# Column sums of all eight squares on TensorE, a re-ordered prologue, and work issued behind named instructions, in a four-layer backbone

## The chip, the cores and the metric

The kernel runs on one core of one Trainium2 chip. The metric is the device time of one execution in microseconds (us). The engines are named as in the profile: PE (TensorE, matrix products; PEld is its weight load), DVE (VectorE), ACT (ScalarE), POOL (GpSimd) and SP (SyncE, which issues most of the DMA transfers).

## What is computed

512 tokens, 256 of context (`ctx`) and 256 latent (`x`), of 1024 channels pass through four layers. Each layer has a token mixer (layer 0 latent attention, layer 1 a Conformer convolution, layer 2 a Hyena long convolution, layer 3 latent attention again) and a gated feed-forward network (FFN) with a convolution over three neighbours. Ahead of each mixer and each FFN the tokens are normed and modulated:

```python
def rmsnorm(x, g):
    y = xf * lax.rsqrt(jnp.mean(xf * xf, axis=-1, keepdims=True) + EPS)
    return (y * g.astype(F32)).astype(x.dtype)
def modulate(x, g, shift, scale):
    return rmsnorm(x, g) * (1 + scale) + shift
...
    sh1, sc1, g1, sh2, sc2, g2 = jnp.split(s_lat @ ada_w[i] + ada_b[i], 6, axis=-1)
    csh1, csc1, cg1, csh2, csc2, cg2 = jnp.split(s_ctx @ ada_w[i] + ada_b[i], 6, axis=-1)
    hl = modulate(x, norm_mix[i], sh1, sc1)
    ...
    x = x + g1 * yl
    x = x + g2 * conv_ffn(modulate(x, norm_ffn[i], sh2, sc2), *ffn)
def conv_ffn(h, w_up, w_dw, b_dw, w_down):
    g = dwconv(a[..., :D_FF], w_dw, b_dw)          # a = h @ w_up
    return (jax.nn.silu(g) * a[..., D_FF:]) @ w_down
```

The shifts and scales are products of the conditioning vectors with `ada_w` (1024 x 6144 for each layer). The Hyena filter (two sine layers, a decay, the discrete Fourier transform of the filter, and the sum of its absolute values by which it is divided) depends on weights alone, so it can be computed at any time before layer 2.

## The kernel before, in words

The tokens are kept transposed, `x[128, KT=8, 512]`: 8 tiles of 128 channels by 512 tokens, the context in columns 0 to 255 (`s=0`), the latent tokens behind (`s=1`). Every float32 operand of a product is split into a high part (ACT copies it rounded, L144, L169, L385) and a low part (DVE subtracts, L147, L170, L166 for `hl`); a product is three matmuls, hi by hi, lo by hi, hi by lo (`mm3`, L158 to L160). Weights come as 1 MB tiles `raw` through SP's queue and are split into `whi` and `wlo`.

The order on PE is written by hand (`tc.manual_schedule`). The order on DVE, ACT, POOL and SP is made by a scheduler from the program's order, priorities, and the buffers that are free when it plans: 35 buffers for tiles `g` and `e`, 4 for `raw`, 11 for `w`, 7 PSUM banks for `mm`. An engine carries its instructions out strictly in that order.

**The prologue** is the time until layer 0's attention begins. It holds: the modulation of layer 0 (`ada_group(0, 0)`, eight slices k of 1 MB of `ada_w`, four products each, L243; k=2 to 4 in two tiles `aw`; one step for each `fill()`); its eviction (ACT L248), four transposes and the bias (`settle()`, L260, L262); the sine layers (`spectra`: products L1144 and L1157, sines L1100 to L1107) with four column products L1151 for the Conformer filter, whose results `ka` go to DRAM (`spill`); the first half of the Hyena filter (`spectra_half(0, ...)`: for two halves t of the filter taps L1171 to L1185, then spectra columns `fcol`, six products each, L1195); the sums of squares of the tokens. `piece()` takes the next step of the last two, and `warm_up(n)` issues n idle products (L221).

For the norm, ACT squares the eight tiles of x (L335), DVE adds the first seven (L337, six adds), and `Norm.sums(s)` multiplies the accumulated tile and the eighth with a column of ones (L357; 128 tokens become one column, four products for each s). ACT adds eps (`tv`, L360), POOL takes the power -1/2 (`rsy`, L195), ACT lays it on a diagonal (L364), PE spreads it over the partitions (L368, `spread`). `Norm.apply(s)` scales x (DVE L166, `e<-x,moda,mm`), adds the shift (ACT L385, `hh`) and takes the low part (`hl`).

**Layer 0's head** (`mla`): four weight tiles `w_c` (two halves of two, `whi`, `wlo`), products of `hh` of the context with them for k = 0 to 7 (L636), `nm.sums(1)` between k=3 and k=4, products of `hl` (L642), the latent tokens' `spread` behind the first eight of these, then the latent tokens' products.

**Each FFN** has 22 units j: six pairs of weight tiles' products (L158 to L160) into two banks, then `post(j)`: a scaled eviction (ACT L528), two taps (DVE L166 `e<-mm,par,e`), silu (L533), the product (DVE L534) and a split (L169, L170). After some units `down(gi)` multiplies back and adds to x (DVE L166 `x<-mm,mod,x`). Beside it `ada_side` computes the next layer's modulation on DVE and ACT: eight products L284 and eight accumulations L285 for each tile. In layer 1's FFN, which is called the second FFN here, the second half of the Hyena filter is computed as well: `spectra_half(1, ...)`, one step every second unit.

Of the kernel before, what the change touches and what calls it, by code (L numbers as in the profile page):

```python
# [16 lines left out]
ALU = mybir.AluOpType  # L17
# [5 lines left out]
T = 512  # L23
# [60 lines left out]
def kernel(ctx: ExitStack, tc: tile.TileContext, xT, cT, cB, ada0, ada2, adaT1, adaT2, adaT3, prm, mlp, w_c, w_ug, w_o,  # L84
# [80 lines left out]
    def stt(o, a, s, b, op0, op1, **kw):  # L165
        nc.vector.scalar_tensor_tensor(out=o, in0=a, scalar=s, in1=b, op0=op0, op1=op1, **kw)  # L166

    def split(hi, lo, src):
        nc.scalar.activation(out=r(hi), in_=src, func=AF.Copy)  # L169
        nc.vector.tensor_tensor(out=r(lo), in0=src, in1=hi, op=ALU.subtract)  # L170

# [58 lines left out]
    def ada_group(li, g, early=False):  # L230
        mod_tile(li)
        ps = pa.tile([P, T], F32, tag="ada", name="ada")
        for k in range(KT):
            if early and k in (2, 3, 4):
                raws = [wp.tile([P, 1024], F32, tag="w", name="aw", bufs=WB) for _ in range(2)]
            else:
                raws = [wp.tile([P, 2048], F32, tag="raw", name="raw", bufs=RAW)]
            n = 4 // len(raws)
            for i, raw in enumerate(raws):
                at = (4 * g + n * i) * T  # L240
                nc.sync.dma_start(out=raw, in_=(ada0, None, ada2)[li][k * P:(k + 1) * P, at:at + n * T])
            for c in range(4):
                nc.tensor.matmul(out=ps[32 * c:32 * c + 32, :], lhsT=spad[:, k, :], rhs=raws[c // n][:, c % n * T:(c % n + 1) * T],  # L243
                                 start=(k == 0), stop=(k == KT - 1))
            if k < KT - 1:
                yield
        sb = e_tile()
        nc.scalar.activation(out=sb, in_=ps, func=AF.Copy)  # L248
        late.append((li, g, sb))
        yield  # L250

    late = []

# [64 lines left out]
    def need(n):  # L318
        while units[0] < n:
            was = units[0]  # L320
            fill()
            if units[0] == was:
                break

    class Sq:
        def __init__(self, c0, eng=nc.gpsimd):
            self.c0, self.acc, self.n, self.parts, self.eng = c0, None, [0, 0], {}, eng

        def add(self, k, a, b):
# [16 lines left out]
    class Norm:  # L346
# [6 lines left out]
        def sums(self, s):  # L353
            ps = ps_tr()
            for t in range(2):
                for i, q in enumerate(self.sq.parts[s]):
                    nc.tensor.matmul(out=ps[:, t:t + 1], lhsT=q[:, s * L + t * P:s * L + (t + 1) * P], rhs=ones[:, 0:1],  # L357
                                     start=i == 0, stop=i == 1)
            v = sp.tile([P, 2], F32, tag="tv", name="tv")
# [10 lines left out]
        def apply(self, s):  # L370
# [5 lines left out]
            if self.a is None:  # L376
                self.a = sp.tile([P, KT, 2], F32, tag="moda", name="moda")
                stt(self.a, self.m[:, self.c + 8:self.c + 16, :], 1.0, self.g.unsqueeze(2).to_broadcast([P, KT, 2]),
                    ALU.add, ALU.mult)
            hs = []  # L380
            shift = lambda k: self.m[:, self.c + k, s:s + 1]
            for k in range(KT):
                hs.append(e_tile()[:, v])
                stt(hs[k], x[:, k, v], self.a[:, k, s:s + 1], R[:, v], ALU.mult, ALU.mult)
                nc.scalar.activation(out=r(HH[:, k, v]), in_=hs[k], func=AF.Identity, bias=shift(k))  # L385
            with tc.high_priority(offset=-18 if s == 0 else 0):
# [194 lines left out]
    def mla(li, nm):  # L581
# [6 lines left out]
        for u in range(2):  # L588
            w += [both(t, lambda a: a.rearrange("p (k c) -> p k c", k=2)) for t in load_w(w_c[j, u], 2 * CW, 2 * CW)]
        if li == layers[0]:  # L590
# [570 lines left out]
    def spectra_half(hc, loaded):  # L1161
# [4 lines left out]
        fwd = lambda t, a, b: (fh[t][:, a:b], fl[t][:, a:b])  # L1166
        ab, asum = [], []
        for t in range(2):
# [11 lines left out]
            split(hl4[0], hl4[1], s)  # L1180
            split(hl4[2], hl4[3], d)
            ab.append(((hl4[0], hl4[1]), (hl4[2], hl4[3])))
            stt(f, f, -1.0, f, ALU.mult, ALU.max)
            stt(b, b, -1.0, b, ALU.mult, ALU.max)
            nc.vector.tensor_tensor(out=f, in0=f, in1=b, op=ALU.add)  # L1185
            asum.append(f)
            yield
        kf = [[e_tile(), e_tile()] for _ in range(2)]
        for fcol, w in ((0, 0), (1, 0), (2, 1), (3, 1)):
# [4 lines left out]
            for j in range(2):  # L1194
                nc.scalar.activation(out=kf[j][f2][:, im * L:(im + 1) * L], in_=ps[:, j * L:(j + 1) * L], func=AF.Copy)  # L1195
            if fcol % 2:
                yield
# [164 lines left out]
    with tc.manual_schedule(engines={mybir.EngineType.PE}):  # L1362
        filler[0] = chain(ada_group(0, 0, True), ada_group(0, 1), ada_group(0, 2), ada_group(2, 0))
        la, lb = spectra_load()
        pieces = chain(spectra(la), spectra_half(0, lb))
        sq = Sq(0, nc.vector)
        nm = Norm(layers[0], 0, sq)
        def piece():
            kas.extend(next(pieces) or ())
# [3 lines left out]
        for k in (0, 4):  # L1373
            nc.sync.dma_start(out=x[:, k:k + 4, :], in_=xT[:, k:k + 4, :])
        for k in range(KT):
            sq.add(k, 0, T)
        for i in range(3):
            piece()
        warm_up(12)
        fill()  # L1380
        for i in range(2):
            piece()
            warm_up(6)
            fill()
        nm.sums(0)
        fill(3)
        piece()
        settle()
        piece()
        nm.apply(0)  # L1390
        spare[0] = pieces
# [168 lines left out]
```

## Time and profile before

| | us |
|---|---|
| median of 3 runs (lowest, highest) | 2145.23 (2144.37, 2145.5) |
| the profiled execution | 2145.16 |
| its span in the profile | 2143.3 |
| PE busy, share of the span | 2096.1, 98% |
| DVE busy, share | 1557.3, 73% |
| ACT busy, share | 1287.5, 60% |
| mean granted clock of PE | 0.994 |

The span is what the rows below divide; 1.86 us of the profiled execution lie outside it. A row of a timeline gives start, duration, engine, line, operation, tiles (output <- inputs) and count, and in brackets how long the engine had stood idle and whose end released it.

### The profile page before, as it was taken

To read this page: it belongs to the slowest core of one execution; us is meant where nothing else is said; L and a number is where in the kernel's file an instruction comes from. 1 tells how busy PE (TensorE), PEld (TensorE's weight loads), DVE (VectorE), ACT (ScalarE), POOL (GpSimd) and SP (SyncE) were. 2 spreads that over 40 slices of the span, in tenths; PEclk is the share of its full clock that TensorE was granted. 3 is DMA by queue.
4 is the path that set the end of the run, shared out by engine and by line. 5 is a ranking of instruction groups with operands and counts; after the bars stand their busy time and mean duration, and the time that the engine had idled before them with its cause. 6 is when DMAs were issued, how large, how long until landed. Compare 5 with 4: busy or idle time off the path is not lost.

```text
span 2143.3 us, 32063 instructions
## 1 busy us (share of the span) xinstructions
PE 2096.1 (98%) x12108; PEld 1801.3 (84%) x12108; DVE 1557.3 (73%) x2780; ACT 1287.5 (60%) x2774; POOL 236.2 (11%) x403
## 2 busy tenths in 40 slices
PE   7999999999999999999999999999999998899999
PEld 5767898888899979888888988898888888669999
DVE  5878368889756665768775689757979856976665
ACT  3788457778644465547654544456868745875453
POOL 0375200000020012000000200020000002621000
PEclk8999999999999999999999999999999999999999
DMA  8533135545432152444542322224545531114552
GB/s 316 211 131 139 60 118 179 214 177 200 173 128 84 59 205 81 155 150 163 196 171 85 114 85 93 99 79 158 210 182 196 197 113 50 58 46 171 180 189 85
DMA packets 48699, 305.39 MB, mean 142 GB/s; under 512 B 5536, under 2 KB 6688, under 8 KB 16160
## 3 DMA queue, kind: packets, MB, share of 16 engines
q1 hardware_dynamic: 47824, 300.91, 39.8%
q8 instruction: 95, 1.56, 0.3%
q10 hardware_dynamic: 720, 2.44, 0.3%
q14 instruction: 60, 0.49, 0.1%
HBM read 299.13 MB, written 4.19 MB: 142 GB/s over the span
## 4 chain that ended last, share of the span: by engine, by line
PE 89%; DVE 4%; ACT 3%; POOL 2%; DMA 1%; issue 1%; SPq 0%; POOLq 0%; ACTq 0%; DVEq 0%
PE mm L158 26%; PE mm L159 25%; PE mm L160 25%; PE mm L463 4%; PE mm L469 2%; PE mm L850 1%; PE ada L243 1%; PE tr L829 1%; PE mm L636 1%; ACT g L761 1%; DMA x<-in_xT_dram 1%; PE tr L357 1%; PE idle L221 1%; POOL e L337 1%; PE mm L642 0%
## 5 line engine op out<-in xcount | busy, mean ns | idle before, releaser
L158 PE MATMUL mm<-hh,whi 128*128 128x512 f32 (+1 forms) x1856 | 657.2, 354 | 0.0
L159 PE MATMUL mm<-hl,whi 128*128 128x512 f32 (+1 forms) x1856 | 654.5, 353 | 0.0
L160 PE MATMUL mm<-hh,wlo 128*128 128x512 f32 (+1 forms) x1856 | 654.2, 352 | 0.0
L147 DVE TENSOR_TENSOR wlo<-raw,whi 128x1024 fp32r<-128x1024 f32 (+2 forms) x361 | 430.0, 1193 | 290.4 <-PE mm L159 179.2
L144 ACT ACTIVATE whi<-raw 128x1024 fp32r<-128x1024 f32 (+3 forms) x370 | 374.6, 1017 | 293.9 <-PE mm L160 160.7
L158 PEld LDWEIGHTS mm<-hh,whi 128*128 128x128 f32 x1856 | 351.1, 189 | 51.7 <-issue 3.1
L160 PEld LDWEIGHTS mm<-hh,wlo 128*128 128x128 f32 x1856 | 351.0, 189 | 47.7
L159 PEld LDWEIGHTS mm<-hl,whi 128*128 128x128 f32 x1856 | 351.2, 189 | 46.3
L285 ACT ACTIVATE e<-e 128x512 f32<-128x512 f32 x512 | 315.9, 619 | 80.8 <-DVE e L284 80.5
L284 DVE TENSOR_TENSOR e<-raw,e 128x512 f32<-128x512 f32 x512 | 315.3, 684 | 0.0
L158 PE MATMUL mm<-g,whi 128*128 128x512 f32 (+1 forms) x904 | 309.1, 342 | 0.0
L159 PE MATMUL mm<-g,whi 128*128 128x512 f32 (+1 forms) x904 | 307.5, 340 | 0.0
L160 PE MATMUL mm<-g,wlo 128*128 128x512 f32 (+1 forms) x872 | 298.5, 342 | 0.0
L337 POOL TENSOR_TENSOR e<-e 128x256 f32<-128x256 f32 (+1 forms) x63 | 70.2, 1114 | 1209.7 <-ACT e L335 1176.6
L158 PEld LDWEIGHTS mm<-g,whi 128*128 128x128 f32 x904 | 171.3, 189 | 19.7
L159 PEld LDWEIGHTS mm<-g,whi 128*128 128x128 f32 x904 | 171.3, 190 | 19.6
L160 PEld LDWEIGHTS mm<-g,wlo 128*128 128x128 f32 x872 | 165.3, 190 | 19.0
L169 ACT ACTIVATE g<-e 128x512 fp32r<-128x512 f32 (+1 forms) x137 | 76.3, 558 | 106.4 <-DVE e L534 45.3
L166 DVE SCALAR_TENSOR_TENSOR e<-mm,par,e 128x510 f32<-128x510 f32 (+3 forms) x186 | 126.2, 678 | 15.6 <-ACT e L528 11.6
L166 DVE SCALAR_TENSOR_TENSOR x<-mm,mod,x 128x256 f32<-128x256 f32 x192 | 85.3, 477 | 52.0 <-PE mm L160 51.8
L170 DVE TENSOR_TENSOR g<-e,g 128x512 fp32r<-128x512 f32 (+1 forms) x137 | 81.9, 598 | 41.8 <-ACT g L169 41.4
L528 ACT ACTIVATE e<-mm,par 128x512 f32<-128x512 f32 (+1 forms) x88 | 63.0, 716 | 63.7 <-PE mm L160 59.2
(264 smaller groups left out, 2856.1 us busy)
## 6 DMA issues: line engine op xcount, KB each, us to landing
raw<-in_w_fup_dram SPq DMA_DIRECT2D x88, 1024.0 KB, 4.9
raw<-in_adaT_dram SPq DMA_DIRECT2D x64, 1024.0 KB, 4.8
raw<-in_w_fd_dram SPq DMA_DIRECT2D x32, 1024.0 KB, 4.9
raw<-in_ada_dram SPq DMA_DIRECT2D x29, 1024.0 KB, 5.2
raw<-in_w_fd_dram SPq DMA_DIRECT2D x16, 768.0 KB, 4.2
raw<-in_w_p_dram SPq DMA_DIRECT2D x12, 1024.0 KB, 4.9
raw<-in_w_hi_dram SPq DMA_DIRECT2D x12, 1024.0 KB, 5.0
raw<-in_w_o_dram SPq DMA_DIRECT2D x8, 1024.0 KB, 4.9
```

The source lines that it names most:

```text
L144: nc.scalar.activation(out=r(hi[:, 0:n]), in_=part, func=AF.Copy)
L147: nc.vector.tensor_tensor(out=r(lo[:, 0:n]), in0=part, in1=hi[:, 0:n], op=ALU.subtract)
L158: nc.tensor.matmul(out=ps, lhsT=r(ah), rhs=r(bh), start=start, stop=False)
L159: nc.tensor.matmul(out=ps, lhsT=r(ah), rhs=r(bl), start=False, stop=False)
L160: nc.tensor.matmul(out=ps, lhsT=r(al), rhs=r(bh), start=False, stop=stop)
L166: nc.vector.scalar_tensor_tensor(out=o, in0=a, scalar=s, in1=b, op0=op0, op1=op1, **kw)
L169: nc.scalar.activation(out=r(hi), in_=src, func=AF.Copy)
L170: nc.vector.tensor_tensor(out=r(lo), in0=src, in1=hi, op=ALU.subtract)
L284: nc.vector.tensor_tensor(out=t, in0=raw[:, q * D + (i % 2) * T:q * D + (i % 2 + 1) * T], in1=sb[i], op=ALU.mult)
L285: nc.scalar.activation(out=t, in_=t, func=AF.Copy, accum_out=asum[:, 2 * u + q, i // 2, i % 2:i % 2 + 1])
L337: self.eng.tensor_tensor(out=self.acc[:, a:b], in0=self.acc[:, a:b], in1=t[:, a:b], op=ALU.add)
L463: nc.tensor.matmul(out=banks[i][q][:, v], lhsT=r(wq[:, k, :]), rhs=r(HH[:, k, v]), start=k == 0 and wq is w[i][q][0], stop=False)
```

## The change

`Sq.all` squares the eight tiles on ACT and hands all eight to `Norm.sums`; the six adds on DVE are gone, and `sums` has 16 products instead of 4 for each s. In the prologue, PE's order is written anew. The splits of the four `w_c` tiles may be issued only behind marked instructions (`tc.issue_after`: the eviction of the modulation and the second scaled tile for the first pair, the last `hh` of the context for the second). In `spectra_half`, for both halves of the filter, the absolute values are issued only behind the last split of t=1 (mark "parts"). In the first half, each spectra column is a step of its own.

```diff
+        def all(self):
+            tiles = []
+            for k in range(KT):
+                tiles.append(e_tile())
+                nc.scalar.activation(out=tiles[k], in_=x[:, k, :], func=AF.Square)
+            self.parts = {0: tiles, 1: tiles}
...
-                for i, q in enumerate(self.sq.parts[s]):
+                qs = self.sq.parts[s]
+                for i, q in enumerate(qs):
                     nc.tensor.matmul(out=ps[:, t:t + 1], lhsT=q[:, s * L + t * P:s * L + (t + 1) * P], rhs=ones[:, 0:1],
-                                     start=i == 0, stop=i == 1)
+                                     start=i == 0, stop=i == len(qs) - 1)
...
-            w += [both(t, lambda a: a.rearrange("p (k c) -> p k c", k=2)) for t in load_w(w_c[j, u], 2 * CW, 2 * CW)]
+            with queued(*((("evict", "scaled"), ("apply",))[u] if li == layers[0] else ())):
+                w += [both(t, lambda a: a.rearrange("p (k c) -> p k c", k=2)) for t in load_w(w_c[j, u], 2 * CW, 2 * CW)]
...
-            split(hl4[2], hl4[3], d)
+            marks["parts"] = split(hl4[2], hl4[3], d).ins
             ab.append(((hl4[0], hl4[1]), (hl4[2], hl4[3])))
-            stt(f, f, -1.0, f, ALU.mult, ALU.max)
-            stt(b, b, -1.0, b, ALU.mult, ALU.max)
-            nc.vector.tensor_tensor(out=f, in0=f, in1=b, op=ALU.add)
-            asum.append(f)
+            fb.append((f, b))
             yield
+        with queued("parts"):
+            for f, b in fb:
+                stt(f, f, -1.0, f, ALU.mult, ALU.max)
+                stt(b, b, -1.0, b, ALU.mult, ALU.max)
+                nc.vector.tensor_tensor(out=f, in0=f, in1=b, op=ALU.add)
+                asum.append(f)
...
-            if fcol % 2:
+            if fcol % 2 or hc == 0:
                 yield
...
-        for k in range(KT):
-            sq.add(k, 0, T)
         for i in range(3):
             piece()
-        warm_up(12)
+        warm_up(10)
+        piece()
+        sq.all()
         fill()
-        for i in range(2):
-            piece()
-            warm_up(6)
-            fill()
+        piece()
+        warm_up(4)
+        fill(2)
         nm.sums(0)
-        fill(3)
         piece()
+        fill()
+        piece()
+        fill(2)
+        warm_up(4)
         settle()
+        nm.spread(0)
+        nm.apply(0)
         piece()
-        nm.apply(0)
+        piece()
         spare[0] = pieces
```

The order on PE around the sums of the context (names: `ada` is the modulation, `aw` and `raw` its slices, `idle` the warm-up, `g` the filter's split parts). Before:

```order
L221 MATMUL idle<-ones,ident 128x128 x6
L243 MATMUL ada<-aw,spad 32x512 x4
L357 MATMUL tr<-ones,e 128x1 x4
L243 MATMUL ada<-raw,spad 32x512 x12
L158 MATMUL mm<-g 128x512
L159 MATMUL mm<-g 128x512
L160 MATMUL mm<-g 128x512
```

Of the change (its L373 is L357 of before):

```order
L243 MATMUL ada<-aw,spad 32x512 x8
L373 MATMUL tr<-ones,e 128x1 x16
L158 MATMUL mm<-g 128x512
L159 MATMUL mm<-g 128x512
L160 MATMUL mm<-g 128x512
L158 MATMUL mm<-g 128x512
L159 MATMUL mm<-g 128x512
L160 MATMUL mm<-g 128x512
L243 MATMUL ada<-raw,spad 32x512 x4
```

The products with ones have grown from 4 to 16 and stand ahead of the last three slices of the modulation; two spectra columns stand among these slices.

The two last spectra columns now stand behind the spread (L384, before L368):

```order
L243 MATMUL ada<-raw,spad 32x512 x8
L221 MATMUL idle<-ones,ident 128x128 x4
L262 MATMUL tr<-ident,e 128x128 x4
L384 MATMUL mm<-e,ones 128x256
L158 MATMUL mm<-g 128x512
```

In before all spectra columns stood ahead of the spread.

The order on ACT up to the context's `hh` (L385). Before:

```order
L144 ACTIVATE whi<-raw 128x832
L364 ACTIVATE e<-ident,rsy 128x128 x2
L248 ACTIVATE e<-ada 128x512
L1195 ACTIVATE e<-mm 128x256 x4
L144 ACTIVATE whi<-raw 128x832 x2
L1195 ACTIVATE e<-mm 128x256 x2
L144 ACTIVATE whi<-raw 128x832
L1195 ACTIVATE e<-mm 128x256 x2
L385 ACTIVATE hh<-e,mod 128x256 x7
```

Of the change (L404 is L385 of before, L1219 is L1195):

```order
L248 ACTIVATE e<-ada 128x512
L144 ACTIVATE whi<-raw 128x832
L404 ACTIVATE hh<-e,mod 128x256 x2
L1219 ACTIVATE e<-mm 128x256
L404 ACTIVATE hh<-e,mod 128x256 x5
L1219 ACTIVATE e<-mm 128x256
L404 ACTIVATE hh<-e,mod 128x256
L1219 ACTIVATE e<-mm 128x256 x2
L144 ACTIVATE whi<-raw 128x832 x3
```

Three of the four splits of `w_c` (`whi`) now stand behind the last of the eight `hh`, and the spectra's copies stand among the `hh`.

The order on DVE in the second FFN, around the last updates of x of its first `down` (`x<-mm`); the last row is the first low part for unit j=10. Before:

```order
L166 SCALAR_TENSOR_TENSOR x<-mm,mod,x 128x256 x6
L170 TENSOR_TENSOR g<-e,g 128x512
L284 TENSOR_TENSOR e<-raw,e 128x512 x15
L166 SCALAR_TENSOR_TENSOR x<-mm,mod,x 128x256
L284 TENSOR_TENSOR e<-raw,e 128x512
L166 SCALAR_TENSOR_TENSOR x<-mm,mod,x 128x256
L284 TENSOR_TENSOR e<-raw,e 128x512 x8
L147 TENSOR_TENSOR wlo<-raw,whi 128x1024
```

Of the change (L554 is L534 of before, L286 is L284, L1210 is L1185):

```order
L554 TENSOR_TENSOR e<-e,mm 128x512
L166 SCALAR_TENSOR_TENSOR x<-mm,mod,x 128x256 x2
L170 TENSOR_TENSOR g<-e,g 128x512
L286 TENSOR_TENSOR e<-raw,e 128x512 x24
L166 SCALAR_TENSOR_TENSOR e<-e 128x512
L166 SCALAR_TENSOR_TENSOR e<-mm,par,e 128x2x255
L1210 TENSOR_TENSOR e<-e 128x512
L166 SCALAR_TENSOR_TENSOR e<-mm,par,e 128x2x255
L147 TENSOR_TENSOR wlo<-raw,whi 128x1024
```

The x updates stand ahead of all 24 products of `ada_side`, and between these and `wlo` there are now an absolute value and a sum (`e<-e`, L1210) and the taps of unit j=9.

## Rows read from the trace of the kernel before

**Rows 1.** the page's first part: busy us, share of the span, instructions:

```profile
PE 2096.1 (98%) x12108; PEld 1801.3 (84%) x12108; DVE 1557.3 (73%) x2780; ACT 1287.5 (60%) x2774; POOL 236.2 (11%) x403
```

**Rows 2.** the middle: length, PE, PEld, DVE, ACT, POOL busy, clock, DMA share, GB/s:

```profile
950.00:1000.00 50.00, 50.00 (x222) 41.42 (x221) 35.07 (x54) 27.65 (x69) 0.00 (x0) 1.00 0.41 139
```

**Rows 3.** chain that ended last: start us, us, what:

```profile
5.30 13.95 DMA x<-in_xT_dram
```

**Rows 4.** timeline, first 64 us: start, us, engine, line, tiles, [idle before]:

```profile
13.31 3.69 PE L1151 MATMUL mm<-w,e 31*128 31x512 f32 x8
...
19.28 2.19 ACT L335 ACTIVATE e<-x 128x512 f32<-128x512 f32 x4 [1.60 <-DMA x<-in_xT_dram]
...
22.14 0.53 DVE L1100 TENSOR_SCALAR e<-tr,par 64x256 f32<-64x256 f32 x1
...
25.04 1.11 PE L1157 MATMUL tr<-e 64*64 64x256 f32 x2 [8.03 <-ACT e L1107]
...
32.15 1.98 PE L1171 MATMUL mm<-w,e 64*128 64x512 f32 x4
...
42.01 2.78 PE L243 MATMUL ada<-raw,spad 128*32 128x512 f32 x24
...
48.33 1.69 ACT L144 ACTIVATE whi<-raw 128x832 fp32r<-128x832 f32 x2
...
49.26 1.96 DVE L147 TENSOR_TENSOR wlo<-raw,whi 128x832 fp32r<-128x832 f32 x2 [0.63 <-ACT whi L144]
...
50.80 0.59 PE L368 MATMUL mm<-e,ones 128*128 128x256 f32 x2
51.22 0.68 ACT L1195 ACTIVATE e<-mm 128x256 f32<-128x256 f32 x2
51.43 3.22 DVE L166 SCALAR_TENSOR_TENSOR e<-x,moda,mm 128x256 f32<-128x256 f32 x8 [0.21 <-PE mm L368]
```

**Rows 5.** timeline from 52 us on:

```profile
51.95 2.91 ACT L385 ACTIVATE hh<-e,mod 128x256 fp32r<-128x256 f32 x7
...
52.51 0.46 PE L636 MATMUL mm<-whi,hh 128*128 128x416 f32 x1 [1.11 <-ACT hh L385]
...
55.65 0.95 PE L357 MATMUL tr<-ones,e 128*128 128x1 f32 x8
...
60.82 0.70 ACT L364 ACTIVATE e<-ident,rsy 128x128 f32<-128x128 f32 x2 [3.19 <-POOL rsy L195]
...
63.60 0.35 PE L636 MATMUL mm<-whi,hh 128*128 128x416 f32 x1
```

**Rows 6.** DMA issues of 20.9 to 22 us: size, us to landing:

```profile
raw<-in_ada_dram SPq DMA_DIRECT2D x1, 1024.0 KB, 14.8
```

**Rows 7.** TensorE's granted clock after its first long idle (columns as Rows 2):

```profile
17.00:18.00 1.00, 0.01 (x1) 0.00 (x0) 0.89 (x2) 0.68 (x2) 0.00 (x0) 0.53 1.08 442
```

**Rows 8.** one line's instructions: ns min/median/max, first and last start, forms:

```profile
L195 POOL TENSOR_TENSOR rsy<-tv,nhalf x15: 707/717/3813, 42.5 to 1946.2; 128x2 f32<-128x2 f32 x15
```

**Rows 9.** timeline of VectorE in the second FFN:

```profile
972.55 9.12 DVE L284 TENSOR_TENSOR e<-raw,e 128x512 f32<-128x512 f32 x15
...
987.79 1.22 DVE L147 TENSOR_TENSOR wlo<-raw,whi 128x1024 fp32r<-128x1024 f32 x1
988.92 1.53 DVE L166 SCALAR_TENSOR_TENSOR e<-mm,par,e 128x510 f32<-128x510 f32 x2
```

**Rows 10.** timeline of TensorE there:

```profile
976.07 0.39 PE L158 MATMUL mm<-hh,whi 128*128 128x512 f32 x1
...
990.12 0.39 PE L160 MATMUL mm<-hh,wlo 128*128 128x512 f32 x1
```

**Rows 11.** timeline of TensorE late in the kernel, its longest wait:

```profile
1832.45 0.45 PE L771 MATMUL tr<-ident,e 128*96 128x128 f32 x1 [5.97 <-DVE e L669]
```

**Rows 12.** clock around that wait (columns as Rows 2):

```profile
1829.00:1830.00 1.00, 0.00 (x0) 0.00 (x0) 1.00 (x4) 0.11 (x1) 0.75 (x3) 0.77 0.00 0
...
1836.00:1837.00 1.00, 1.00 (x7) 0.73 (x5) 0.21 (x2) 0.79 (x3) 0.76 (x4) 0.82 1.04 147
```

More of the change, by code (lines that the diff above doesn't have):

```diff
@@ L165, in stt @@
     def stt(o, a, s, b, op0, op1, **kw):
-        nc.vector.scalar_tensor_tensor(out=o, in0=a, scalar=s, in1=b, op0=op0, op1=op1, **kw)
+        return nc.vector.scalar_tensor_tensor(out=o, in0=a, scalar=s, in1=b, op0=op0, op1=op1, **kw)
     def split(hi, lo, src):
         nc.scalar.activation(out=r(hi), in_=src, func=AF.Copy)
-        nc.vector.tensor_tensor(out=r(lo), in0=src, in1=hi, op=ALU.subtract)
+        return nc.vector.tensor_tensor(out=r(lo), in0=src, in1=hi, op=ALU.subtract)
     def rsqrt_seed(eng, v, n, tag):
@@ L247, in ada_group @@
         sb = e_tile()
-        nc.scalar.activation(out=sb, in_=ps, func=AF.Copy)
+        evict = nc.scalar.activation(out=sb, in_=ps, func=AF.Copy)
         late.append((li, g, sb))
+        if (li, g) == (0, 0):
+            marks["evict"] = evict.ins
         yield
-    late = []
+    late, marks = [], {}
     def settle():
@@ L323, in need, with queued @@
                 break
+    def queued(*names):
+        st = ExitStack()
+        for n in names:
+            st.enter_context(tc.issue_after(marks[n]))
+        return st
     class Sq:
@@ L383, in apply @@
                 hs.append(e_tile()[:, v])
-                stt(hs[k], x[:, k, v], self.a[:, k, s:s + 1], R[:, v], ALU.mult, ALU.mult)
-                nc.scalar.activation(out=r(HH[:, k, v]), in_=hs[k], func=AF.Identity, bias=shift(k))
+                y = stt(hs[k], x[:, k, v], self.a[:, k, s:s + 1], R[:, v], ALU.mult, ALU.mult)
+                if k == 1:
+                    marks.setdefault("scaled", y.ins)
+                hi = nc.scalar.activation(out=r(HH[:, k, v]), in_=hs[k], func=AF.Identity, bias=shift(k))
+            marks.setdefault("apply", hi.ins)
             with tc.high_priority(offset=-18 if s == 0 else 0):
@@ L1166, in spectra_half @@
         fwd = lambda t, a, b: (fh[t][:, a:b], fl[t][:, a:b])
-        ab, asum = [], []
+        ab, asum, fb = [], [], []
         for t in range(2):
@@ L1365 @@
         pieces = chain(spectra(la), spectra_half(0, lb))
-        sq = Sq(0, nc.vector)
+        sq = Sq(0)
         nm = Norm(layers[0], 0, sq)
```

## Prediction

> **What bounds the kernel now.** I read the page's first part before all else: PE is busy for 98% of the span, DVE for 73%, ACT for 60% [rows 1]. In the middle PE never idles, at full clock [rows 2], so there a change counts only by PE's own passes or by a wait that it makes for PE. Two places where PE does wait are touched by the change: the prologue, and (through the scheduler) the second FFN.
>
> In the chain of waits the kernel begins with the transfer of x, which lands at 19.25 [rows 3]. The timeline shows why that matters: ACT's second four squares start then, DVE's six adds stand ahead of its first sine layer, so L1100 starts only at 22.14, and PE, done with L1151 at 17.00, waits 8.03 us until L1157 at 25.04 [rows 4]. Everything of the filter is late by that, up to the spread of the context's norm at 50.80 (call this moment S) [rows 4]. From S to the first product of the latent tokens at 63.60 [rows 5] are 12.8 us. I measure the prologue by that last moment: behind it the two kernels do the same work.
>
> **The prologue up to S.** Without the adds, the first sine layer runs from 13.4 (L1151 starts at 13.31, right behind its input's product). It takes 2.9 us, from L1100 to L1157 [rows 4], and ends under L1151. So L1157 goes at 17.0, the second layer ends at 17.0 + 1.1 + 2.9 = 21.0, the taps L1171 of t=0 at 23.0 (1.98). In PE's new order follow slice k=2 (24 rows of L243 took 2.78 at full clock, eight cost 0.93; I take 1.0), t=1 (2.0), idle passes (1.0) and k=3, 4 (2.0): 29.0. The squares now stand on ACT behind the splits of t=0. Those wait for five operations of DVE from 22.0 on (0.6 to 0.7 each, like L284 on tiles of the same shape [rows 9]): with two splits of 0.55 they end at 26.3, and eight squares (2.19 for four [rows 4]) at 30.7. The products with ones: four instructions of before are eight L357 rows, two passes each, and took 0.95 [rows 5], 0.119 a pass. The context's 16 are 32 passes; half of them come behind the last square: 30.7 + 16 x 0.12 = 32.6. Spectra column 0 then waits for `tv` on ACT (0.3), ACT's split of t=1 (0.6) and DVE's low part (0.7), with half its products behind these (0.7): 34.9. A product of 512 columns takes 0.227 (62 of them from 976.07 to 990.12 [rows 10]), so k=5 (1.0), column 1 (1.4), k=6 and 7 (1.9) end at 39.2. The eviction (0.6, a tile like a square's) with its hand-overs ends at 40.2, the idle passes beside it; transposes 0.6 (512 columns, like L368): **S at 40.8**, 10.0 earlier.
>
> DMA allows that: the slice of `ada_w` issued at about 21 took 14.8 [rows 6], so the last is there at 35.8, ahead of column 1's end. It also sets the floor: 35.8 + 1.0 product + 0.6 eviction + 0.8 transposes and bias = 38.2.
>
> **The prologue behind S.** Here the change gives back. Two spectra columns (12 products, 2.8) now stand between the spread and the first `hh` product, which in before came at S + 1.7 [rows 5]. The splits of `w_c` were done there ahead of S (two `whi` 1.69, two `wlo` 1.96 [rows 4]); now they queue behind the scaling. DVE scales from S + 0.63 for 3.22 [rows 4], takes the first `wlo` by S + 4.9; PE has k=0, 1 by S + 6.25. ACT starts its `hh` at S + 1.15, writes eight (2.91 for seven [rows 5]) and copies four spectra halves (0.68 for two [rows 4]) by S + 5.8, splits the second tile by S + 6.7, DVE by S + 7.8; PE has k=2, 3 by S + 9.15, which in before was S + 4.85. The latent sums cost 32 passes at 0.119 (0.95 for eight [rows 5]), 3.8 for 0.95: S + 12.95. Sixteen products (16 from 52.51 to 55.65 [rows 5], 0.19 each) 3.05, eight `hl` products 1.5, spread 0.35, eight more 1.5: S + 19.4 (19.75 with a wait for the spread), against 12.8. Later by 6.6 to 6.95, so the prologue gains 10.0 - 6.95 to 10.0 - 6.6, 3.05 to 3.4.
>
> Ends for the unknown: with S on its floor and no hand-over lost, 3.4 + 2.6, less 0.2, about 5.8. At the other end PE's first gap may cost the clock. [...] In the change PE still has a gap between L1157 and the taps, filled only by ten idle products. Half speed up to the sums would cost 1 to 2, and a slow `rsy` 0.4 more (below): 0. I take **-2.5**.
>
> L195 of POOL had a median of 717 ns and once 3813 [rows 8]. The long one is this one: `y` was ready at 60.82 after 3.19 us of ACT waiting [rows 5]. From the sums' end to that of the diagonals were 4.92 (56.60 to 61.52). If it is as long again, the spread comes at S + 12.95 + 4.92 = S + 17.9 where PE asks at S + 17.5; at the median PE waits for nothing. I take the median, for at S + 13.4 DVE has its `hl` behind it.
>
> [...]
>
> The weight of a pass with one output column is the other disputed price. The row gives 0.119 [rows 5], so 24 more passes cost 2.85 on PE. [...] The row decides: each pass comes with a weight load of its own, 128 x 128. With the floor the time would be 2149.3, still in the forecast's own case; I give that 0.02 of its chance.
>
> **The second FFN.** The order on PE is the same here, but DVE's and ACT's are not. The mark "parts" holds f and b of both halves t until the last split of t=1, so the pool is short of buffers, and the scheduler moved the splits of t=1, the taps of unit j=8 and the last x updates ahead of the 24 products L284. In before, 15 of the 24 ran from 972.55 for 9.12 [rows 9], 0.608 each, while PE was still in the first `down`. PE began unit j=9 at 976.07 and j=10's first `wlo` product at 990.12 [rows 10]; that `wlo` had been written from 987.79 for 1.22 [rows 9]: it was ready 1.1 us before PE wanted it. That is all the cover there is.
>
> In the change the last x update waits for the end of `down`, 976.07, and ends with the product L554 ahead of it and the split behind it at 978.8. Then 24 x 0.608 = 14.6: 993.4. Then an absolute value (0.6), a tap (1.53 for two [rows 9], 0.77), the sum (0.6), a tap (0.77): 996.1, and `wlo` 1.2: 997.2. ACT's `whi` comes behind 24 accumulations of the same length, no later than that. PE asks at 990.12: it waits **7.1**. At least 5.7: from 976.07 with nothing but the 24 products, absolute value, taps, sum and `wlo`, 2 x 0.6 + 1.53 + 1.2 + 14.6 less overlaps, 19.8, is 995.9. If ACT or a buffer holds DVE, 7.5.
>
> To this comes the clock. [...] So PE ran 3.9 us at half speed, a loss of 1.9. Lower end 0. **Second FFN: +9.0** (5.7 to 9.5). It isn't caught up: PE is the bound from there on [rows 2].
>
> **Other parts, at nothing.** The idle products (24 to 18) fill gaps. `ka_d` in SP's queue now stands between the two `w_c` pairs, each far ahead of its split; if not, the cover is the 12 spectra products, 2.8. Layers 2 and 3 have their orders as before.
>
> **Sum.** 2143.3 - 2.5 + 9.0 = 2149.8 span, with 1.86 outside 2151.6. The profiled execution, 2145.16, lies 0.07 below the median. Forecast **2151.5**, slower by 0.3%. A change of 0.2% (4.3 us) is about what a measurement of this kernel can tell from none.
>
> **Rivals.**
> - *Worse* (0.16): the prologue gains nothing (clock at half in the first gap, slow L195) and the wait is there: 2145.2 + 9 to 10 = 2154 to 2155.5. For it: the half clock of [rows 7]. Against: ten idle products stand in the gap.
> - *Small stall* (0.20): PE waits 5.7, the clock holds, the prologue gains 3 to 5.8: 2145 to 2148. [...] Against: [rows 12] at the same length.
> - *No wait in the second FFN* (0.14), the other side: the scheduler's planned order matters only if DVE is late, and if x updates and taps run earlier than I count, the 24 products begin at 972 as in before. The prologue alone then decides: 2139.5 to 2143, faster by over 0.2% if its gain passes 4.3, that is S before about 39.9 with the rest as counted. Against: the last update can't precede 976.07.
> - *The change isn't made on the chip as written* I give nothing: the order shows it.
>
> The forecast's own case (2148.5 to 2153.5) has 0.50. Range 2143.5 to 2155.0: it leaves out the good half of the third rival and the end of the first. Slower: the forecast's case nearly whole (0.47) and the first rival (0.16): 0.63. Faster 0.07, the same 0.30.
>
> **What would show each step.** S near 41 and the latent tokens' first L636 near 60 to 61.5. The sums between k=3 and k=4: 32 rows of 3.8. L1100 at 13.4. L195 at 0.7. In the second FFN a PE wait of 6 to 7 ahead of j=10's first products, `wlo` behind 24 L286, granted clock below 1 for some 4 us after. Wrong would make it: no such wait, another wait of PE behind 100 us that the order doesn't show, or S above 44.

## The result, and the profile after

The changed kernel takes 2157.3 us (median of 4 runs, 2155.36 to 2159.12) where the kernel before took 2144.8 beside it (4 runs): ratio 1.0056, 95% interval 1.0044 to 1.0068. It is slower, as forecast, but by 12 us instead of 6.5, and 2.3 us outside the range. The profiled execution took 2155.36, the least of the four; its span is 2153.5, 10.2 more than before, and its mean granted clock 0.992. The other three show 0.989 or 0.990.

The page's first part shows next to nothing: PE has 11.7 us more, DVE 4.6 less (beside [rows 1]).

```profile
PE 2107.8 (98%) x12144; PEld 1807.5 (84%) x12144; DVE 1552.7 (72%) x2774; ACT 1287.6 (60%) x2774; POOL 232.5 (11%) x403
```

The timeline of the changed kernel's prologue, beside [rows 4, 5] (L1121 is L1100 of before, L1178 L1157, L1192 L1171, L373 L357, L384 L368, L657 L636):

```profile
13.41 0.54 DVE L1121 TENSOR_SCALAR e<-tr,par 64x256 f32<-64x256 f32 x1 [7.90 <-PE tr L1165]
...
16.92 0.64 PE L1178 MATMUL tr<-e 64*64 64x256 f32 x2
...
20.51 1.98 PE L1192 MATMUL mm<-w,e 64*128 64x512 f32 x4 [0.51 <-ACT e L1128]
...
29.01 4.05 PE L373 MATMUL tr<-ones,e 128*128 128x1 f32 x32
32.92 0.77 PE L158 MATMUL mm<-g 128*128 128x512 f32 x1
...
43.18 0.60 PE L384 MATMUL mm<-e,ones 128*128 128x256 f32 x2
...
48.11 0.46 PE L657 MATMUL mm<-wlo,hh 128*128 128x416 f32 x1 [1.41 <-DVE wlo L147]
...
50.69 0.46 PE L657 MATMUL mm<-wlo,hh 128*128 128x416 f32 x1 [0.61 <-DVE wlo L147]
...
52.13 3.63 PE L373 MATMUL tr<-ones,e 128*128 128x1 f32 x32
...
56.13 0.70 POOL L195 TENSOR_TENSOR rsy<-tv,nhalf 128x2 f32<-128x2 f32 x1 [21.91 <-ACT tv L376]
...
56.72 0.55 PE L657 MATMUL mm<-whi,hh 128*128 128x416 f32 x1
...
63.73 0.35 PE L657 MATMUL mm<-whi,hh 128*128 128x416 f32 x1
```

The sine layer starts at 13.41, as worked out, and the spread (S) comes at 43.18 instead of 50.80. Yet the latent tokens' first product starts at 63.73, 0.13 *later* than before. What was in neither sum of the prediction shows in the length of the products: behind each series of 32 one-column passes, a product of 512 columns takes 0.6 to 0.8 and one of 416 takes 0.55, where 0.39 and 0.35 are usual. The stretches of the same profile (columns as Rows 2) show why:

```profile
31.00:32.00 1.00, 1.00 (x11) 1.00 (x10) 0.00 (x0) 0.00 (x0) 0.00 (x0) 1.00 1.07 442
32.00:33.00 1.00, 1.00 (x8) 1.00 (x7) 0.00 (x0) 0.00 (x0) 0.00 (x0) 0.63 0.96 401
33.00:34.00 1.00, 1.00 (x4) 0.80 (x4) 0.09 (x1) 0.90 (x3) 0.49 (x1) 0.50 0.98 406
...
56.00:57.00 1.00, 1.00 (x5) 0.96 (x4) 0.00 (x0) 0.19 (x2) 0.70 (x1) 0.58 0.92 364
57.00:58.00 1.00, 1.00 (x4) 0.95 (x4) 0.00 (x0) 1.00 (x4) 0.00 (x0) 0.50 0.18 70
```

PE is busy for all of each microsecond, and the clock falls from 1.00 to 0.50. By the shares in these rows the first fall begins at 32.3, while the last passes of the first series run, and lasts until 39; the second begins at 56.2, just behind the second series, and lasts until 59.6. PE does one-column passes right ahead of both. Its last waits are 0.51 us ahead of 20.51 for the first fall, 1.41 and 0.61 us ahead of 48.11 and 50.69 for the second; the kernel a_fb0_wide below has the same three waits (0.51, 1.39 and 0.61) and no such fall.

In the second FFN VectorE and TensorE run as the order said:

```profile
980.28 14.54 DVE L286 TENSOR_TENSOR e<-raw,e 128x512 f32<-128x512 f32 x24
...
997.54 1.23 DVE L147 TENSOR_TENSOR wlo<-raw,whi 128x1024 fp32r<-128x1024 f32 x1 [0.16 <-ACT whi L144]
```

```profile
997.56 0.80 PE L158 MATMUL mm<-hh,whi 128*128 128x512 f32 x1 [6.11 <-ACT whi L144]
...
998.82 0.80 PE L160 MATMUL mm<-hh,wlo 128*128 128x512 f32 x1
```

```profile
994.00:995.00 1.00, 0.00 (x0) 0.00 (x0) 1.00 (x3) 1.00 (x4) 0.00 (x0) 0.91 0.20 82
...
1000.00:1001.00 1.00, 1.00 (x4) 0.81 (x3) 1.00 (x2) 1.00 (x3) 0.00 (x0) 0.50 0.00 0
1001.00:1002.00 1.00, 1.00 (x4) 0.76 (x4) 1.00 (x2) 0.93 (x1) 0.00 (x0) 0.68 0.81 106
```

All 24 products stand ahead of `wlo` and none ahead of the x updates (beside [rows 9]); PE waits 6.11 us for `whi` ahead of unit j=10, comes to the first `wlo` product at 998.82 (beside [rows 10]) and has half the clock until 1001.6 (beside [rows 12]).

The account of this execution goes by markers that both traces have. Latent tokens' first product: +0.13. Layer 1's transposes at 765: -0.04. Unit j=9's end: +1.62. The second filter half's sum, which DVE takes at 1039.17 before and 1049.32 after: +10.15. The end: +10.2. So 8.5 us are lost in the second FFN and 1.6 between 769 and 773, a place that the change doesn't touch. The sum's rows before and after, then the stretches at 769 and the products there:

```profile
1039.17 0.16 DVE L1211 TENSOR_SCALAR rn<-tr 128x4 f32<-128x4 f32 x1 [0.31 <-PE tr L1208]
```

```profile
1049.32 0.16 DVE L1235 TENSOR_SCALAR rn<-tr 128x4 f32<-128x4 f32 x1 [1.75 <-PE tr L1232]
```

```profile
769.00:770.00 1.00, 1.00 (x10) 0.33 (x12) 0.96 (x3) 1.00 (x3) 0.00 (x0) 0.77 0.47 197
770.00:771.00 1.00, 1.00 (x12) 0.36 (x8) 0.84 (x4) 1.00 (x4) 0.00 (x0) 0.50 0.02 8
```

```profile
769.30 3.47 PE L243 MATMUL ada<-raw,spad 128*32 128x512 f32 x16
```

There, PE has done 24 transposes of 98 columns, without a wait, when the clock falls; 16 products of the modulation then take 3.47 instead of 1.92.

### The profile page after: what moved, and what is told of

Its sections match the earlier page's. It is cut to its first block, busy times and chain, and to the rows that moved or that the text cites. A ratio compares the mean times of both kernels' runs of the same rounds, so it can differ in the third digit from the quotient of the medians.

```text
span 2153.5 us, 32132 instructions
## 1 busy us (share of the span) xinstructions
PE 2107.8 (98%) x12144; PEld 1807.5 (84%) x12144; DVE 1552.7 (72%) x2774; ACT 1287.6 (60%) x2774; POOL 232.5 (11%) x403
## 4 chain that ended last, share of the span: by engine, by line
PE 89%; DVE 4%; ACT 4%; POOL 1%; issue 1%; DMA 1%; SPq 0%; ACTq 0%; POOLq 0%; DVEq 0%
PE mm L158 25%; PE mm L159 25%; PE mm L160 25%; PE mm L483 4%; PE mm L489 2%; PE mm L871 1%; PE ada L243 1%; PE mm L657 1%; PE tr L850 1%; PE tr L373 1%; ACT g L782 1%; PE mm L663 1%; DVE e L166 1%; ACT g L833 1%; POOL e L352 1%
## 5 line engine op out<-in xcount | busy, mean ns | idle before, releaser
L286 DVE TENSOR_TENSOR e<-raw,e 128x512 f32<-128x512 f32 x512 | 315.1, 685 | 0.0
```

Of the source, the lines that this page charges most:

```text
L286: nc.vector.tensor_tensor(out=t, in0=raw[:, q * D + (i % 2) * T:q * D + (i % 2 + 1) * T], in1=sb[i], op=ALU.mult)
```

## The experiments

Theory: two losses. One is the order in the second FFN, caused by the delayed absolute values of the filter's second half. The other is the clock behind the one-column passes, which eats the prologue's gain. Rivals: the prologue alone is at fault; the clock falls for PE's gaps or the place of the work, not for the passes' width. Each result gives the median of its runs, their lowest and highest, and the ratio to the kernel before, run on the same chip beside it, with its 95% interval; a difference of two ratios, times 2145, is given as us.

**The delay alone, in the kernel before (b_fb1).**

`magnitude` holds the three operations of before: two absolute values and their sum.

```diff
...
+            fb.append((f, b))
+            if hc == 0:
+                magnitude(f, b)
             yield
+        if hc:
+            with tc.issue_after(parts):
+                for f, b in fb:
+                    magnitude(f, b)
```

> The kernel before with one part of the change alone: the absolute values of the filter's second half issued behind the last split of t=1. Theory (this delay re-orders DVE and ACT in the second FFN, and PE waits for the high and low part of unit j=10): a PE wait of 5.5 to 6.5 us ahead of unit j=10, granted clock 0.5 for some 4 us behind it, and 7.5 to 9 us more than the kernel before, near 2153.3. Rival (the loss comes from the prologue, and what is lost in the second FFN is caught up or would be lost anyway): within 2 us of the kernel before, under 2147.

Measured: 2157.28 (2152.47 to 2157.47, 5 runs), 1.0045 (1.0033 to 1.0058), 9.7 us by the ratio. The wait of the changed kernel is there, behind the prologue of the kernel before:

```profile
999.34 0.80 PE L158 MATMUL mm<-hh,whi 128*128 128x512 f32 x1 [6.11 <-ACT whi L144]
```

The delay alone makes it. In the profiled execution (2157.47), from the end of unit j=9 to the second half's sum, 8.9 us more pass than before. It also has the fall of the clock in layer 1 (768.8 to 775.6), and 3.1 us more are lost between the prologue and that unit: the five runs lie in two groups, 2152.5 to 2153.4 and 2157.3 to 2157.5.

**The changed kernel without that delay (a_fb0).**

```diff
             fb.append((f, b))
+            if hc:
+                magnitude(f, b)
             yield
-        with queued("parts"):
-            for f, b in fb:
...
+        if hc == 0:
+            with queued("parts"):
+                for f, b in fb:
+                    magnitude(f, b)
```

> The changed kernel without that part: the absolute values of the second half stand where they stood before; those of the first half stay delayed. Theory: the wait ahead of unit j=10 and the half clock behind it are gone, 7.5 to 9 us less than the changed kernel: 2148 to 2150, and 2147 if the fall of the clock in layer 1's mixer at 769 us doesn't come back. The prologue ends where it ended in the changed kernel, the latent tokens' first product near 63.9. Rival (the loss is the prologue's): above 2154.

Measured: 2148.79 (2145.88 to 2151.89, 11 runs), 1.0014 (1.0005 to 1.0023). That is 8.5 below the changed kernel by the medians and 9.0 by the ratios, the loss that the account gave. PE has no wait there, and the prologue is as bad as ever; its stretches and its last row:

```profile
32.00:33.00 1.00, 1.00 (x7) 1.00 (x6) 0.00 (x0) 0.00 (x0) 0.00 (x0) 0.53 0.98 410
...
56.00:57.00 1.00, 1.00 (x4) 0.95 (x5) 0.00 (x0) 0.26 (x1) 0.64 (x1) 0.50 0.97 379
```

```profile
63.93 0.35 PE L657 MATMUL mm<-whi,hh 128*128 128x416 f32 x1
```

**The same passes with 128 columns (a_fb0_wide).**

```diff
-                    nc.tensor.matmul(out=ps[:, t:t + 1], ..., rhs=ones[:, 0:1],
+                    nc.tensor.matmul(out=ps[:, t * P:(t + 1) * P], ..., rhs=ones,
...
-            nc.scalar.activation(out=v, in_=ps[:, 0:2], ...)
+            nc.scalar.activation(out=v, in_=ps[:, 0:2 * P:P], ...)
```

> As a_fb0, but the products with ones take all 128 columns of the ones tile instead of one, in as many passes with as many weight loads; column 0 of the result is read. Theory (PE's granted clock falls because the 64 one-column passes of the two sums give TensorE too little to do, though it counts as busy): the clock stays at 1.00 between 32 and 39 us and between 55 and 60 us, the passes take no longer than 0.12 each, the latent tokens' first product comes 4 to 5.5 us sooner, near 59, and the time is 4 to 6 us below a_fb0, at or just below the kernel before. Rival (the clock falls for PE's gaps or for the place of this work, whatever the width): the same falls of the clock, time within 1 us of a_fb0.

Measured: 2143.21 (2140.61 to 2145.4, 11 runs), 0.9992 (0.9983 to 1.0001), 4.7 us below a_fb0 by the ratios. The profiled execution (2140.61) is the fastest of the eleven and has no fall of the clock before 1810. The clock stays up in the same stretches, and the prologue ends 4.62 us sooner:

```profile
32.00:33.00 1.00, 1.00 (x12) 1.00 (x11) 1.00 (x3) 0.00 (x0) 0.00 (x0) 1.00 0.96 401
33.00:34.00 1.00, 1.00 (x7) 0.83 (x6) 1.00 (x3) 0.26 (x1) 0.43 (x1) 1.00 1.05 435
...
56.00:57.00 1.00, 1.00 (x7) 0.99 (x6) 0.00 (x0) 0.00 (x0) 0.00 (x0) 1.00 0.92 352
```

```profile
40.33 0.60 PE L384 MATMUL mm<-e,ones 128*128 128x256 f32 x2
...
49.26 3.73 PE L373 MATMUL tr<-ones,e 128*128 128x128 f32 x32
...
59.31 0.35 PE L657 MATMUL mm<-whi,hh 128*128 128x416 f32 x1
```

128 times the columns cost 0.1 us in 32 passes (3.73 for 3.63). S is 40.33, where 40.8 was worked out.

**One part alone again: 32 passes in the kernel before, narrow and wide (b_sums32, b_sums32_wide).** The added products multiply by zeros, so the sums stay the same.

```diff
+                n = 8 if self.li == layers[0] and self.c == 0 else 2
+                for i in range(n):
+                    q = qs[0] if i < n - 1 else qs[1]
                     nc.tensor.matmul(..., rhs=ones[:, 0:1] if i in (0, n - 1) else spad[:, 0, 2:3], ...)
```

> The kernel before with 16 instead of 4 products with ones for each of layer 0's two first sums; the twelve added ones multiply by a column of zeros, so that the sums stay the same. Theory (narrow passes cost their weight load and then the clock): 0.12 for each of 48 more passes, 5.7 us, and half clock for some us behind each series: 7 to 11 us more than the kernel before, 2152 to 2156. Rival (the passes cost, the clock doesn't fall): 4.5 to 6 us more. Rival (passes hidden behind other waits): under 3 us more.

> As b_sums32 (the kernel before with 32 instead of 8 passes in each of layer 0's two first sums), but each product takes 128 columns: the ones, or zeros for the added ones. Theory (narrow passes lower the clock, their number alone costs 0.12 each): both series take 3.6 to 3.9 us, no fall of the clock behind them where b_sums32 had 0.5 in 42 to 50 and 60 to 64 us, and the prologue ends 3 to 6 us sooner than in b_sums32 (latent tokens' first product near 68 to 70 against 72 to 74). Rival (the place or the length of the series lowers the clock): the same falls, no difference.

Measured: narrow 2158.3 (2156.36 to 2159.81, 5 runs), 1.0057 (1.0045 to 1.007), 12.2 us, more than expected; wide 2154.26 (2152.03 to 2156.16, 5 runs), 1.0037 (1.0025 to 1.005), 7.9 us. In both the first series begins between 40 and 41. The narrow one, then the wide one:

```profile
42.00:43.00 1.00, 1.00 (x10) 1.00 (x9) 0.33 (x1) 0.00 (x0) 0.00 (x0) 0.85 0.00 0
43.00:44.00 1.00, 1.00 (x6) 1.00 (x7) 0.00 (x0) 0.00 (x0) 0.00 (x0) 0.50 0.00 0
```

```profile
43.00:44.00 1.00, 1.00 (x12) 1.00 (x10) 1.00 (x2) 0.74 (x1) 0.00 (x0) 1.00 0.00 0
...
60.00:61.00 1.00, 1.00 (x4) 0.95 (x4) 1.00 (x3) 0.00 (x0) 0.00 (x0) 0.50 0.76 297
```

Here the clock falls *within* the first narrow series and not in the wide one. Both kernels then have a fall ahead of the second series, behind a wait of PE (1.71 us in the narrow one, 3.07 in the wide one). Behind the second series the narrow one falls again, the wide one (last row) doesn't:

```profile
66.00:67.00 1.00, 1.00 (x8) 1.00 (x8) 0.00 (x0) 0.26 (x1) 0.00 (x0) 0.80 0.99 228
67.00:68.00 1.00, 1.00 (x4) 0.96 (x4) 0.00 (x0) 0.19 (x2) 0.69 (x1) 0.50 1.09 408
```

```profile
66.00:67.00 1.00, 1.00 (x7) 0.99 (x7) 0.00 (x0) 0.48 (x2) 0.49 (x1) 1.00 1.02 434
```

The latent tokens begin at 74.68 and 71.70, 3.0 apart, both later than expected.

One rival is left by single pairs of profiles: that the series' place in time, which differs between executions, makes the fall. All profiled executions together speak against it. Each of the eight series of 32 narrow passes (in the changed kernel, a_fb0, a_fill and b_sums32) has a fall that begins within it or less than 0.5 us behind it. None of the eleven series of 32 wide passes has one (a_fb0_wide and the two kernels made from it below, a_wide, b_sums32_wide, and the first series of a_best), though the clock falls elsewhere in most of these executions.

**Do the two losses add up? (a_wide)** The changed kernel with the wide sums, the delay left in.

> The changed kernel with the sums' products at 128 columns and nothing else, the delayed absolute values of the second half included. If the two losses add up (prologue's clock, wait in the second FFN): 4 to 6 us below the changed kernel's 2157.3, 2151 to 2153, with a PE wait of 6 us ahead of unit j=10 and the latent tokens' first product near 59. If one hides the other: under 2 or over 8 us below.

Measured: 2152.47 (2148.99 to 2153.61, 7 runs), 1.0028 (1.0017 to 1.0039), 4.8 below the changed kernel by the medians, 6.0 by the ratios. The latent tokens begin at 59.53, and the wait is the same:

```profile
993.49 0.80 PE L158 MATMUL mm<-hh,whi 128*128 128x512 f32 x1 [6.10 <-ACT whi L144]
```

**The clock's share of the second FFN's loss (a_fill).**

```diff
             if j > 1:
+                if li == 1 and j == 10:
+                    warm_up(26)
                 w = load(j)
```

> The changed kernel with 26 idle products (52 passes of 128 columns, 5.6 us at full clock) ahead of unit j=10 of the second FFN, where PE waited 6.1 us. Theory (of the 8 us lost there some 2 are the half clock behind the wait): the wait shrinks to under 1 us, the granted clock stays at 1.00 behind it, unit j=10 starts where it did, and what follows comes 1.5 to 2.5 us sooner; 2155 to 2156 where the changed kernel takes 2157.3. Rival (the clock costs nothing there): the same time, or more by the passes that stick out.

Measured: 2154.83 (2153.28 to 2160.96, 5 runs), 1.0046 (1.0032 to 1.0059), 2.5 below the changed kernel by the medians, 2.1 by the ratios. These intervals overlap, but the trace shows the term by itself: hardly a wait, then the full clock. From the last product ahead of unit j=10 (and of the idle ones) to that unit's 41st product 16.52 us pass, where they are 17.82 in the changed kernel: 1.3 less, a little under what was expected.

```profile
997.72 5.97 PE L221 MATMUL idle<-ones,ident 128*128 128x128 f32 x52
1003.98 0.50 PE L158 MATMUL mm<-hh,whi 128*128 128x512 f32 x1 [0.30 <-ACT whi L144]
```

```profile
1006.00:1007.00 1.00, 1.00 (x6) 0.79 (x6) 1.00 (x2) 1.00 (x2) 0.00 (x0) 1.00 0.00 0
```

The profiled execution, 2160.96, came late to all this, and that tells something of the changed kernel, whose code it has up to unit j=10. Its clock was at 0.50 from 14.5 to 24.8, which the profiled execution of the changed kernel (1.00 there) doesn't show:

```profile
14.00:15.00 1.00, 1.00 (x3) 0.35 (x3) 0.93 (x3) 0.00 (x0) 0.00 (x0) 0.76 1.03 418
```

The first sums begin at 32.60 instead of 29.01, and the latent tokens' first product at 69.18 instead of 63.73.

**Eight narrow passes, by adds on POOL (a_fb0_pool).**

```diff
+                if 0 < k < KT - 1:
+                    nc.gpsimd.tensor_tensor(out=tiles[0], in0=tiles[0], in1=tiles[k], op=ALU.add)
-            self.parts = {0: tiles, 1: tiles}
+            self.parts = {s: (tiles[0], tiles[KT - 1]) for s in range(2)}
```

> As a_fb0, but POOL adds the first seven squares up and the sums have four narrow products for each half of the tokens again, 8 passes instead of 32. Theory (it is the number of narrow passes in a row that lowers the clock): the clock stays up behind both sums, as in the kernel before, the second sums take 1.0 instead of 3.6, and the latent tokens' first product comes 3 to 7 us sooner than in a_fb0, between 57 and 61; 4 to 7 us below a_fb0. POOL's six adds at 1.1 to 1.2 each put the first sums at 34 to 35. Rival (clock falls for PE's gaps): half clock in 33 to 39 as in a_fb0, time within 2 us of a_fb0.

Measured: 2149.59 (2146.76 to 2151.25, 9 runs), 1.002 (1.001 to 1.003). Missed for another reason: the six adds took 8.66 us, to 36.59, so that PE waited for the first sums, and the clock fell in that wait:

```profile
36.64 1.86 PE L375 MATMUL tr<-ones,e 128*128 128x1 f32 x8 [7.03 <-POOL e L343]
```

Behind the second sums, eight narrow passes that PE didn't wait for, the clock stayed at 1.00 (58 to 61), which agrees with the theory; the first tell nothing.

**Without the marks ahead of the splits (a_fb0_wide_nowq).** The `with queued(...)` around the `w_c` splits is taken out.

> As a_fb0_wide, without the marks behind which the w_c splits are issued. If those marks cost what I counted (the first low part behind eight scaled tiles), PE's waits of 1.39 and 0.61 us for wlo are gone and the latent tokens' first product comes up to 2 us sooner, near 57.5. If the marks pay (they keep the splits from delaying the filter's parts), the second spectra column and with it the spread come 0.5 to 2 us later and the time is the same or longer.

Measured: 2142.69 (2141.06 to 2146.09, 11 runs), 0.9986 (0.9977 to 0.9995); latent tokens at 59.36 against 59.31, and S at 42.95 against 40.33. These two profiles don't compare as they stand: here the clock was at 0.50 from 17.0 to 23.8, and the first sums began at 30.98 instead of 29.28. The profile of a_best (below), which has the marks and a fall from 15.7 to 22.5, is the nearer one up to S: sums at 30.91, S at 42.20. So without the marks S comes some 0.75 later, and the way from S to the latent tokens is 16.41 instead of 18.98, 2.6 shorter, the two waits for `wlo` being gone. That makes a gain of about 1.8, an estimate from three profiles; the ratios have 1.3, within overlapping intervals. The marks are not shown to pay, and may cost.

**Layer 1's fall of the clock (a_fb0_wide_hold, b_shift).** One adds `warm_up(10)` behind layer 1's first transposes, the other makes the kernel before's `warm_up(12)` a `warm_up(20)`.

> As a_fb0_wide, with ten idle products (20 passes of 128 columns) between the transposes and the modulation's products in layer 1's mixer, where the clock fell to 0.5 at 769 us in several profiles. Theory (the fall comes from a stretch of products that give TensorE little to do, as with the narrow sums): the passes cost 1.1 us and keep the clock at 1.00 there; against a_fb0_wide, whose times of 2140.6 to 2145.4 I take for runs without and with that fall, the median is 1 to 2.5 us less and the scatter smaller. Rival (something else lowers it): a fall there all the same, median 1 us more.

> The kernel before with 20 instead of 12 idle products ahead of the modulation's third slice, so that all that follows moves back by 1 to 3.5 us (16 passes at 0.11 or 0.21) with the same work. Theory (the fall of the clock in layer 1's mixer hangs on where that stretch lies in time, not on the change): in some runs 1.7 or 3.4 us more than the shift, so a scatter of 3 to 5 us. Rival (the kernel before is free of it, whatever its place): all runs within 1 us of each other, 1 to 3.5 us above the kernel before.

Measured: hold 2146.57 (2143.57 to 2148.87, 11 runs), 1.0003 (0.9994 to 1.0012), 2.4 *more* than a_fb0_wide by the ratios. The theory has no support from it: the clock had fallen ahead of the idle passes, which then ran at half speed.

```profile
764.00:765.00 1.00, 1.00 (x7) 0.64 (x6) 0.78 (x3) 1.00 (x4) 0.00 (x0) 0.96 0.99 418
765.00:766.00 1.00, 1.00 (x5) 0.63 (x4) 0.84 (x3) 1.00 (x3) 0.00 (x0) 0.50 0.82 344
```

```profile
766.13 4.63 PE L221 MATMUL idle<-ones,ident 128*128 128x128 f32 x20
```

The shifted kernel: 2152.34 (2147.34 to 2154.37, 11 runs), 1.0026 (1.0017 to 1.0035). In its profiled execution (2147.83) the spread of the latent tokens came 1.86 us later, and the clock didn't fall in layer 1. The median lies 4.5 above that execution; where the longer runs lose it no profile shows. So eight idle products in the prologue cost this kernel about 2 us in one run and almost 9 in another.

**Both losses taken out, and more (a_best).** As a_fb0_wide, with the latent half of the squares added on POOL, so that the sums between k=3 and k=4 are 8 passes.

> As a_fb0_wide, but POOL, idle until 33 us, adds up the latent half of the first seven squares (six adds of 128x256 at about 1.1 us), so that the sums between k=3 and k=4 take 8 passes instead of 32. Theory (behind the spread PE's own passes set the end of the prologue): 2.7 us sooner at the latent tokens' first product, near 56.6 against 59.3, and 2 to 3 us off the median of a_fb0_wide, to 2140 to 2141.5. Rival (PE then waits for the second pair's wlo, POOL or the spread, or the clock falls): at most 1 us less.

Measured: 2141.12 (2139.46 to 2144.08, 11 runs), 0.998 (0.9971 to 0.9989): 4.3 us faster than the kernel before by the ratio, 2.6 below a_fb0_wide. The profiled execution's latent tokens begin at 58.59, later than expected: the clock was at 0.50 from 15.7 to 22.5, and the first sums began 1.63 later than in a_fb0_wide (30.91 for 29.28). Behind S the way is 16.39 for 18.98, 2.6 shorter, where the theory had 2.7.

## Why the prediction was wrong, point by point

- **The sum.** The forecast had -2.5 for the prologue and +9.0 for the second FFN, 6.5 in all. The profiled execution has +0.1 and +8.5, and 1.6 in layer 1's mixer, 10.2 in all; the median lies 2 us higher still.
- **The prologue up to S** was right but for the clock. DVE's start (13.41), the end of the sums (33.06 for 32.6) and, in a_fb0_wide, S at full clock (40.33 for 40.8) came as worked out. In the changed kernel S is 43.18.
- **The prologue behind S** was right in the same way: 19.4 to 19.75 worked out, 18.98 at full clock (59.31 - 40.33), 20.55 in the changed kernel. No run shows the floor under the price of a one-column pass with which the 2149.3 and its chance of 0.02 are reckoned: 32 passes took 3.63, 0.113 each, close to the row's 0.119.
- **The failed step is the sentence on the clock**: "PE still has a gap between L1157 and the taps [...] Half speed up to the sums would cost 1 to 2 [...] I take -2.5". The clock's price was looked for at that gap alone. The gap was 0.51 us and lowered nothing in the profiled run. The falls came with the sums, which I had priced at 0.12 a pass and at full clock, with nothing for what they do to the products behind them. The width experiment puts that price at 4.4 to 4.6 us in that run (first latent product 63.73 or 63.93 against 59.31). With it, a gain of 4.3 is a loss of 0.1. The end "0" of the range was right, its reason wrong.
- **The row behind that sentence** was read for more than it shows. In [rows 7] the mean of 0.53 for 17 to 18 puts the fall at about 17.1, where PE had only just stopped (L1151 ends at 17.00), so that hardly any idling stands ahead of it. Of the nine profiled kernels with the changed prologue, six show a fall that begins between 14.5 and 17.6, while PE is busy and ahead of the place of the gap (a_fill's is shown above); the changed kernel, a_fb0 and a_fb0_wide don't. What lowers the clock there stays open.
- **L195** took 0.70 (from 56.13), as assumed. DVE ran nothing then (54.10 to 58.11). The one of 3.81 in the kernel before (56.97 to 60.78) ran beside DVE's eight `hl` operations (55.51 to 58.76) and two splits behind them, and one of 2.10 there (from 1793.16) beside `hl` too (until 1793.83). What makes them long is not shown.
- **The second FFN** was right. PE was 1.62 late on its way there, so that without a wait the first `wlo` product would have come at 990.12 + 1.62 = 991.74. It came at 998.82, 7.1 later, as worked out. One detail differs: `whi` was to come no later than DVE, but DVE had to wait 0.16 for it. The clock took 1.4 more behind that (seven products in 3.0 us) for 1.9; 8.5 in all for 9.0. The 1.9 is half of the 3.9 us that PE, in the trace of before, ran at 0.50 behind its wait of 5.97: from 1832.45 [rows 11] to about 1836.4, by the mean of 0.82 for 1836 to 1837 [rows 12]. Both experiments that move this part alone agree (9.7 and 9.0 by the ratios). The wait's lower end was added up wrongly: the terms given for 19.8 make 18.5, so that it should have been 4.5 and not 5.7. That the scheduler's new order comes from the buffers held longer was argued; the runs show only that the delay makes it.
- **The rest of the error** is 1.6 us in the profiled execution and some 2 more in the median. The prediction had the other parts at nothing and gave the clock no term there. The 1.6 are clock lost in layer 1's mixer. The change isn't needed for that fall: b_fb1, b_sums32 and b_sums32_wide, with the prologue of before, have it too, and a_best hasn't. The other three executions show a lower mean clock (0.989 or 0.990 for 0.992) but have no profile, so where they lose the 2 us isn't shown; layer 1 and the stretch from 14.5 on, as in a_fill, are places where it can happen. b_shift shows that a mere shift of the kernel before can raise its median by more than the shift, and a_fb0's runs scatter over 6 us. That layer 1's fall hangs on where that stretch lies is my reading of it. What lowers the clock there stays open; the one try to hold it up failed.
- Of the rivals, *Worse* came closest: no gain in the prologue and the full wait. Its reasons, the first gap and a slow L195, were not what happened in the profiled execution.

## What to carry to other kernels

Read a column sum on TensorE by what it does to the clock behind it as well as by its passes: here two series of 32 one-column passes, 7.3 us by themselves at full clock, cost 4.4 to 4.6 more through the clock, and the same passes with 128 columns, which take nearly the same time, didn't. A scheduling hint must be followed to every place that runs the same code: written for the prologue, it cost 9 us some 950 us later, and the instruction order showed it before any run. Where the clock of a stretch falls in some executions and not in others, differences of 2 to 4 us between kernels need many runs before they say anything of a change.

## What the runs showed of the hardware

- A pass with a 128 x 128 weight load took 0.113 us with one output column and 0.117 with 128, at full clock (3.63 and 3.73 for 32).
- The clock fell to 0.50 while PE was busy for all of every microsecond: late in or just behind 32 narrow passes in the changed kernel (32.3 and 56.2), within them in b_sums32 (42.7), behind transposes of 98 columns in layer 1 (769.5), and in a_fill while products with weights of 31 rows ran (14.5).
- Where it falls differs from execution to execution: a_fill's, whose code is that of the changed kernel up to unit j=10, also fell at 14.5 and 130.6, where the changed kernel's stayed at 1.00. The times of one kernel scatter by 6.0 us in a_fb0 and 7.0 in b_shift (11 runs each); what makes them do so no run here shows.
- POOL's add of two 128x512 tiles took 1.44 us each in a row of six (8.66), one of 128x256 1.02 (6.09).
